# Gates scaled one stage ahead, and the merged product added in DRAM, in a retention and SSD hybrid block

## The chip, the cores and the metric

The kernel runs on one core of one Trainium2 chip. The metric is the device time of one execution in microseconds (us), as the median of several runs.

## The reference

One layer on x of 512 positions by 2048 channels, all in float32. A normalized x is projected to the inputs of two branches and to two gates. The retention branch gives y_r (2048 channels), the SSD branch y_s (4096 channels, normalized over its channels). What the change touches is the end:

```
y_s = rmsnorm(y_s * silu(z), ssd_norm_w)
p_r = y_r @ w_br_ret          # 2048 -> 2048
p_s = y_s @ w_br_ssd          # 4096 -> 2048
merged = sigmoid(gate_r) * p_r + sigmoid(gate_s) * p_s
x = x + merged @ w_out        # 2048 -> 2048
return rmsnorm(x, norm_f_w)
```

The kernel doesn't scale y_s by its norm's root before the product. Since the root R2 depends on the position alone, it multiplies the gate instead: sigmoid(gate_s) * R2 * p_s.

## The kernel before

Activations lie with channels on the 128 partitions and the 512 positions along the row. A float32 product is made of three fast ones: each operand is split into a high part (a cast to float32r) and a low part (the difference), for weights by `split` (L147: ScalarE writes whi, L148; VectorE writes wlo, L149), for activations by `first_half` and `second_half` (L169 and L179), which leave the operands a0 to a7 and b0 to b7.

A **unit** (`unit`, L258) makes 256 output channels from 2048 input channels: eight **slabs** of 256 input channels each. Weights come in pairs of slabs (wf, L235, SyncE's queue, three buffers). In most units a seven-product scheme (Strassen-like, `SEVEN`) is used, for which VectorE makes three differences per pair (L238, L240, L241); units 0 and 7 of the stages discussed here (`PLAIN2`) use the plain scheme. Each slab has 21 matmuls of 128 x 256 in a seven-product unit; the first five slabs run one after the other, the last three group by group (groups of 9, 6 and 6). Units alternate between the PSUM tiles pb and att. At a unit's end ScalarE and VectorE gather the products into o (L269 to L278).

The last four stages each have eight units (two output tiles, called rows, j = 2i and 2i + 1, to a unit):

- the retention product, whose rows are multiplied by the gate gr_d and stored to m_d (L714, L715);
- **half 1** of the SSD product (input channels 0 to 2047), whose rows are stored to ps_d (L726); ahead of it R2 is computed (L718, L719, and L310 to L314);
- **half 2** (channels 2048 to 4095), L728 to L742: for each row SyncE loads ps_d, gs_d (the sigmoid gate) and m_d into tiles f; GpSimd multiplies the gate by R2 (L737); VectorE adds the product to ps (L738), multiplies by the gate (L739) and adds m (L740); ScalarE's queue stores the result to mm_d (L742). The last two rows stay in SBUF;
- the output projection, whose operands are mm_d's rows (L743, loaded by L205), with L173 to L176 for the first halves and L182 to L187 for the second.

The tile f is shared by all loads of these stages and has four buffers; a load waits until the buffer's last user is done, and where that is a store, until it has landed. It stands meanwhile at the head of SyncE's queue:

```
def rtile(src, j, t=None):
    if t is None:
        t = bp.tile([P, T], F32, name="f", tag="f", bufs=4)
    SP.dma_start(out=t, in_=src[j * P:(j + 1) * P, :])
    return t
```

A scheduler in the framework sets the order of each engine's instructions when the program is built, from its own model of times and from priorities (weights go ahead). Each engine, and each queue of transfers, works in that order. The names stay, but the orders move wherever the code changes.

Of the kernel before, what the change touches and what calls it, by code (L numbers as in the profile page):

```python
# [8 lines left out]
F32 = mybir.dt.float32  # L9
# [3 lines left out]
ALU = mybir.AluOpType  # L13
# [3 lines left out]
P = 128  # L17
T = 512
TB = T // P
D = 2048  # L20
# [4 lines left out]
SW = 4096  # L25
# [75 lines left out]
NP = KD // 2  # L101
# [26 lines left out]
def hybrid_block(tc, A, out):  # L128
    nc = tc.nc
    PE, ACT, DVE, POOL, SP = nc.tensor, nc.scalar, nc.vector, nc.gpsimd, nc.sync  # L130
# [6 lines left out]
    op = ctx.enter_context(tc.tile_pool(name="op", bufs=2))  # L137
    dp = ctx.enter_context(tc.tile_pool(name="dp", bufs=1, space=DRAM))
# [5 lines left out]
    def att_tile():  # L144
        return att.tile([P, T], F32, name="att")
# [11 lines left out]
    def raw_tile(i):  # L157
        R[i] = hp.tile([P, 6, 256], F32, name=f"r{i}", tag=f"b{i}")
        return R[i][:, 0:4, :].rearrange("p (r h) t -> p r (h t)", r=2)
# [9 lines left out]
    def first_half(i, DVE=DVE, ACT=ACT):  # L169

        f, t = R[i], hp.tile([P, 8, 256], F32R, name=f"a{i}", tag=f"a{i}")
        X[i] = [t, None]
        DVE.tensor_tensor(f[:, 4, :], f[:, 0, :], f[:, 1, :], op=ALU.subtract)  # L173
        ACT.copy(t[:, 0:4, :], f[:, 1:5, :])
        yield
        DVE.tensor_tensor(t[:, 4:8, :], f[:, 1:5, :], t[:, 0:4, :].bitcast(F32), op=ALU.subtract)  # L176
        yield
# [12 lines left out]
    def second_halves(room):  # L190
        for i in range(NP):
            list(second_half(i, room[i % 2]))
# [4 lines left out]
    def rows(src, i):  # L197
        return src[i * 256:(i + 1) * 256, :].rearrange("(r p) t -> p r t", p=P)

    def load_operands(src, n=NP):  # L200


        for i in range(NP):
            if i < n:
                SP.dma_start(out=raw_tile(i), in_=rows(src, i))  # L205
            list(first_half(i))
# [90 lines left out]
    gs_d = dp.tile([D, T], F32, name="gs_d")  # L297
    ps_d = dp.tile([D, T], F32, name="ps_d")
    m_d = dp.tile([D, T], F32, name="m_d")
    mm_d = dp.tile([D, T], F32, name="mm_d")  # L300
    A_d = dp.tile([SH, T], F32, name="A_d")
    E_d = dp.tile([SH, T], F32, name="E_d")

# [3 lines left out]
    def inverse_root(dst, ps, y, z, n, DVE=DVE, ACT=ACT):  # L307


        ACT.activation(y, ps, AF.Abs_reciprocal_sqrt, scale=1.0 / n, bias=eps)  # L310
        DVE.tensor_scalar(z, ps, 1.0 / n, EPS, op0=ALU.mult, op1=ALU.add)
        DVE.tensor_tensor(dst, y, y, op=ALU.mult)
        DVE.scalar_tensor_tensor(dst, dst, -0.5, z, op0=ALU.mult, op1=ALU.mult)
        DVE.scalar_tensor_tensor(dst, dst, 1.5, y, op0=ALU.add, op1=ALU.mult)  # L314

    bg_ctx = ExitStack()
# [75 lines left out]
    ps = att_tile()  # L392
# [98 lines left out]
    with tc.tile_pool(name="ret", bufs=1) as rp:  # L491
# [3 lines left out]
        for h in range(NH):  # L495
# [45 lines left out]
            for sb in range(TB):  # L541
                n = T - sb * P
                ps = att_tile()
                for i in range(2):
                    PE.matmul(ps[:, :n], k[:, i, sb * P:(sb + 1) * P], q[:, i, sb * P:], start=(i == 0), stop=(i == 1))  # L545
                t = pts[:, (4 * sb - sb * (sb - 1) // 2) * P:][:, :n]
# [10 lines left out]
            for lb in range(TB):  # L557
                ps = att_tile()
# [22 lines left out]
    with tc.tile_pool(name="ssd", bufs=1) as sp:  # L581
# [23 lines left out]
        def gates(off, dst, i):  # L605
            w = w_in[:, off + i * 256:off + (i + 1) * 256]
            for e, x in enumerate(unit([w], plain=(2 * i + (off == GSO)) in PLAIN_M)):
                ACT.activation(x, x, AF.Sigmoid)
                ACT.dma_start(out=dst[(2 * i + e) * P:(2 * i + e + 1) * P, :], in_=x)

        todo = [(o, d, i) for i in range(NG) for o, d in ((GRO, gr_d), (GSO, gs_d))]
        for g in range(NG):
# [3 lines left out]
            ps = att_tile()  # L616
# [3 lines left out]
            ps = att_tile()  # L620
# [6 lines left out]
            for jj in range(2):  # L627
# [5 lines left out]
                for e in range(2):  # L633
                    j = j0 + e
# [7 lines left out]
                    ps = att_tile()  # L642
                    for c in range(TB):
# [6 lines left out]
                                       op=ALU.mult)  # L650
                    ps = att_tile()
# [5 lines left out]
                    for c in range(1, TB - 1):  # L657
                        for i in range(2):
# [8 lines left out]
                                 in_=A_d[hs, :].partition_broadcast(P))  # L667
# [27 lines left out]
                    gates(*todo.pop(0))  # L695
        gates(*todo.pop(0))
    sst_ctx.close()


    with tc.tile_pool(name="br", bufs=1) as bp:  # L700
        def rtile(src, j, t=None):
            if t is None:
                t = bp.tile([P, T], F32, name="f", tag="f", bufs=4)
            SP.dma_start(out=t, in_=src[j * P:(j + 1) * P, :])
            return t

        load_operands(yr_d)
        for i in range(NP):
            if i == 1:
                second_halves([bp.tile([P, 3, 256], F32, name="g", bufs=2) for n in range(2)])  # L710
            for e, x in enumerate(unit([w_r[:, i * 256:(i + 1) * 256]], i % 2, i in PLAIN2)):
                j = 2 * i + e
                t = rtile(gr_d, j)
                DVE.tensor_tensor(t, t, x, op=ALU.mult)  # L714
                ACT.dma_start(out=m_d[j * P:(j + 1) * P, :], in_=t)  # L715
        R2 = R1
        ps = att_tile()
        PE.matmul(ps, ones, R1, start=True, stop=True)  # L718
        inverse_root(R2, ps, *(bp.tile([P, T], F32, name="f", tag="f", bufs=4) for i in range(2)), SW)  # L719
        load_operands(ys_d[:D, :])  # L720
        for i in range(NP):
            if i == 1:
                second_halves([bp.tile([P, 3, 256], F32, name="g", bufs=2) for n in range(2)])
            for e, x in enumerate(unit([w_s[:D, i * 256:(i + 1) * 256]], i % 2, i in PLAIN2)):
                j = 2 * i + e
                ACT.dma_start(out=ps_d[j * P:(j + 1) * P, :], in_=x)  # L726
        load_operands(ys_d[D:, :])
        for i in range(NP):  # L728
            if i == 1:
                second_halves([bp.tile([P, 3, 256], F32, name="g", bufs=2) for n in range(2)])  # L730
            if i == NP - 1:
                last = raw_tile(i)
            for e, x in enumerate(unit([w_s[D:, i * 256:(i + 1) * 256]], i % 2, i in PLAIN2)):
                j = 2 * i + e
                p = rtile(ps_d, j, last[:, e, :] if i == NP - 1 else None)
                s, m = rtile(gs_d, j), rtile(m_d, j)
                POOL.tensor_tensor(s, s, R2, op=ALU.mult)  # L737
                DVE.tensor_tensor(p, p, x, op=ALU.add)  # L738
                DVE.tensor_tensor(p, p, s, op=ALU.mult)  # L739
                DVE.tensor_tensor(p, p, m, op=ALU.add)  # L740
                if i < NP - 1:
                    ACT.dma_start(out=mm_d[j * P:(j + 1) * P, :], in_=p)  # L742
        load_operands(mm_d, NP - 1)  # L743
    bg_ctx.close()


    with tc.tile_pool(name="fin", bufs=1) as fp:
# [4 lines left out]
        for i in range(NP - 1):  # L752
            if i == 1:
                second_halves([xo[n].rearrange("p r (h t) -> p (r h) t", h=2)[:, 0:3, :] for n in (5, 6)])
            t = xo[i]
            SP.dma_start(out=t, in_=rows(A["xT"], i))
            for e, x in enumerate(unit([w_o[:, i * 256:(i + 1) * 256]], i % 2, i in PLAIN2)):
                j = 2 * i + e
# [9 lines left out]
        t = xo[NP - 1]  # L768
        for e in range(2):
            j = KD - 1 - e  # L770
# [4 lines left out]
        ps = [att_tile()[:, :256] for h in halves]  # L775
# [78 lines left out]
```

## Time and profile before

| | |
|---|---|
| time, median of 3 runs | 2753.27 us (2751.96 to 2756.13) |
| the profiled execution's own time | 2755.9 us |
| its span | 2754.0 us |
| granted TensorE clock, mean | 0.993 |
| moved by DMA | 362.46 MB, 132 GB/s in the mean |

PE is TensorE's matmuls and PEld its weight loads, DVE is VectorE, ACT ScalarE, POOL GpSimd, SP SyncE; a q behind a name is that engine's queue, in which transfers are issued and waits are stood out. "x <- y" after a group names who ended most of its idle time. Rows of windows give a stretch, its length, then the busy time and count of each engine, the granted clock, the share of DMA and GB/s. Times in rows are us from the start of the span.

### The profile page before, as it was taken

The numbers are of one execution on the slowest core, as the hardware profiler recorded it, in microseconds if no ns is written. First come the engines' busy times: TensorE is split into PE (matmuls) and PEld (weight loads), VectorE is DVE, ScalarE is ACT, GpSimd is POOL, SyncE is SP. The second block draws the span as 40 slices with busy tenths as digits, with TensorE's granted clock in tenths as the row PEclk, the third lists the DMA queues.
The fourth block names the chain that finished last, engine by engine and source line by source line (L and its number), as shares of the span: only waits on it lengthen the run. The fifth ranks groups of instructions, "written<-read, shape, count | busy, mean of one in ns | idle before, by whom it ended". The sixth has DMA issues, their size and how long they took to land.

```text
span 2754.0 us, 51975 instructions
## 1 busy us (share of the span) xinstructions
PE 2691.5 (98%) x20448; PEld 2565.0 (93%) x20448; DVE 2368.3 (86%) x3799; ACT 1342.7 (49%) x1923; POOL 179.3 (7%) x130
## 2 busy tenths in 40 slices
PE   7999999999999999999999999999999999999998
PEld 4899999999999999999999999999999999898897
DVE  7998888888869898888989898898989897898997
ACT  4434333433345555565565555566564353433443
POOL 0000000000000000000000000000000000011221
PEclk9999999999999999999999999999999999999999
DMA  4223333333333444343444434343464644557534
GB/s 156 85 89 108 100 104 104 104 93 104 104 113 121 129 129 129 107 129 114 131 127 134 138 107 125 119 136 121 129 202 154 212 140 131 176 182 226 193 120 138
DMA packets 339766, 362.46 MB, mean 132 GB/s; under 512 B 25152, under 2 KB 297792, under 8 KB 339520
## 3 DMA queue, kind: packets, MB, share of 16 engines
q1 hardware_dynamic: 319136, 325.05, 38.2%
q10 hardware_dynamic: 20384, 34.09, 3.3%
q8 instruction: 160, 2.62, 0.4%
q14 instruction: 86, 0.70, 0.1%
HBM read 321.56 MB, written 37.49 MB: 130 GB/s over the span
## 4 chain that ended last, share of the span: by engine, by line
PE 78%; DVE 9%; DMA 6%; issue 3%; ACT 1%; SPq 1%; POOL 0%; DVEq 0%; ACTq 0%; POOLq 0%
PE pb L223 21%; PE pb L221 21%; PE pb L222 21%; DMA wf<-in_w_in_dram 3%; DVE wlo L149 3%; PE att L222 2%; PE att L223 2%; PE att L221 2%; PE att L545 1%; DVE wf L238 1%; PE att L560 1%; PE att L677 1%; DMA wf<-in_w_br_ssd_dram 1%; PE att L681 1%; PE pb L118 1%
## 5 line engine op out<-in xcount | busy, mean ns | idle before, releaser
L148 ACT CAST whi<-wf 128x896 fp32r<-128x896 f32 (+1 forms) x968 | 817.6, 884 | 908.2 <-PE pb L222 370.4
L149 DVE TENSOR_TENSOR wlo<-wf,whi 128x896 fp32r<-128x896 f32 (+1 forms) x968 | 988.3, 1033 | 57.2 <-ACT whi L148 35.6
L221 PE MATMUL pb<-a,whi 128*128 128x256 f32 (+1 forms) x3328 | 998.3, 303 | 7.7 <-DVE o L277 4.3
L223 PE MATMUL pb<-a,wlo 128*128 128x256 f32 (+1 forms) x3328 | 994.5, 301 | 7.2 <-DVE wlo L149 7.1
L222 PE MATMUL pb<-a,whi 128*128 128x256 f32 (+1 forms) x3328 | 996.8, 300 | 0.0
L221 PEld LDWEIGHTS pb<-a,whi 128*128 128x128 f32 x3328 | 636.0, 191 | 32.3 <-issue 7.4
L223 PEld LDWEIGHTS pb<-a,wlo 128*128 128x128 f32 x3328 | 635.2, 191 | 30.4 <-DVE wlo L149 8.9
L222 PEld LDWEIGHTS pb<-a,whi 128*128 128x128 f32 x3328 | 637.1, 191 | 20.3 <-issue 0.2
L221 PE MATMUL pb<-b,whi 128*128 128x256 f32 x2112 | 600.1, 284 | 0.0
L223 PE MATMUL pb<-b,wlo 128*128 128x256 f32 x2112 | 599.0, 284 | 0.0
L222 PE MATMUL pb<-b,whi 128*128 128x256 f32 x2112 | 598.1, 284 | 0.0
L238 DVE TENSOR_TENSOR wf<-wf 128x512 f32<-128x512 f32 x400 | 286.1, 715 | 173.9 <-DMA wf<-in_w_in_dram 133.0
L221 PEld LDWEIGHTS pb<-b,whi 128*128 128x128 f32 x2112 | 405.8, 192 | 0.1
L222 PEld LDWEIGHTS pb<-b,whi 128*128 128x128 f32 x2112 | 405.8, 192 | 0.0
L223 PEld LDWEIGHTS pb<-b,wlo 128*128 128x128 f32 x2112 | 405.5, 192 | 0.2
L241 DVE TENSOR_TENSOR wf<-wf 128x256 f32<-128x256 f32 x400 | 174.9, 437 | 3.2
L240 DVE TENSOR_TENSOR wf<-wf 128x256 f32<-128x256 f32 x400 | 174.3, 436 | 3.5
L223 PE MATMUL att<-a,wlo 128*128 128x256 f32 (+1 forms) x480 | 144.5, 306 | 5.1 <-DVE wlo L149 5.1
L221 PE MATMUL att<-a,whi 128*128 128x256 f32 (+1 forms) x480 | 145.2, 305 | 0.0
L222 PE MATMUL att<-a,whi 128*128 128x256 f32 (+1 forms) x480 | 145.2, 305 | 0.0
L223 PEld LDWEIGHTS att<-a,wlo 128*128 128x128 f32 x480 | 90.8, 192 | 10.3 <-DVE wlo L149 6.5
L221 PEld LDWEIGHTS att<-a,whi 128*128 128x128 f32 x480 | 92.0, 192 | 3.9
(217 smaller groups left out, 2731.5 us busy)
## 6 DMA issues: line engine op xcount, KB each, us to landing
wf<-in_w_in_dram SPq DMA_DIRECT2D x640, 256.0 KB, 3.1
wf<-in_w_br_ssd_dram SPq DMA_DIRECT2D x128, 256.0 KB, 3.3
wf<-in_w_out_dram SPq DMA_DIRECT2D x72, 256.0 KB, 3.1
wf<-in_w_in_dram SPq DMA_DIRECT2D x128, 128.0 KB, 2.6
L<-A_d SPq DMA_DIRECT2D x32, 512.0 KB, 3.7
wf<-in_w_br_ret_dram SPq DMA_DIRECT2D x64, 256.0 KB, 3.4
ys_d<-B ACTq DMA_DIRECT2D x32, 256.0 KB, 2.0
r<-ys_d SPq DMA_DIRECT2D x16, 512.0 KB, 6.6
```

Source lines behind the costliest of these rows:

```text
L118: ins = getattr(self.engine, name)(*args, **kw).ins
L148: ACT.copy(dst_hi, src)
L149: DVE.tensor_tensor(dst_lo, src, dst_hi.bitcast(F32), op=ALU.subtract)
L221: PE.matmul(o, wh, xh, start=b not in started, stop=False, skip_group_check=True)
L222: PE.matmul(o, wh, xl, start=False, stop=False, skip_group_check=True)
L223: PE.matmul(o, wl, xh, start=False, stop=(k == NP - 1), skip_group_check=True)
L238: DVE.tensor_tensor(f2[:, :, 4:6, :], f2[:, :, 1:3, :], f2[:, :, 0:1, :].to_broadcast([P, 2, 2, P]), op=ALU.subtract)
L240: DVE.tensor_tensor(f2[:, :, 0, :], f2[:, :, 2, :], f2[:, :, 4, :], op=ALU.add)
L241: DVE.tensor_tensor(f2[:, :, 6, :], f2[:, :, 3, :], f2[:, :, 0, :], op=ALU.subtract)
L545: PE.matmul(ps[:, :n], k[:, i, sb * P:(sb + 1) * P], q[:, i, sb * P:], start=(i == 0), stop=(i == 1))
L560: PE.matmul(ps[:, :DK], pt[sb][:, (lb - sb) * P:(lb - sb + 1) * P], v[:, sb, :], start=(sb == 0), stop=(sb == lb))
L677: PE.matmul(pi[i * 64:(i + 1) * 64, c * P:(c + 1) * P], xd[:, c, i, :], L[:, i, c, :], start=True, stop=True)
```

## The change

Four edits. The product gate * R2 moves from half 2 to half 1: there each row's gate is loaded, multiplied by GpSimd and stored back to gs_d through ScalarE's queue. In half 2 the rows 0 to 13 are no longer added to m by VectorE and stored to mm_d; GpSimd's queue writes them to m_d by a transfer that adds to what lies there. mm_d is gone, and the output projection reads m_d. Rows 14 and 15 load m and are added on VectorE as before. The tile f has six buffers in place of four, and the pool bg is closed ahead of these stages.

```
-    mm_d = dp.tile([D, T], F32, name="mm_d")
...
     sst_ctx.close()
+    bg_ctx.close()
...
-                t = bp.tile([P, T], F32, name="f", tag="f", bufs=4)
+                t = bp.tile([P, T], F32, name="f", tag="f", bufs=6)
...
                 ACT.dma_start(out=ps_d[j * P:(j + 1) * P, :], in_=x)
+
+                s = rtile(gs_d, j)
+                POOL.tensor_tensor(s, s, R2, op=ALU.mult)
+                ACT.dma_start(out=gs_d[j * P:(j + 1) * P, :], in_=s)
...
                 p = rtile(ps_d, j, last[:, e, :] if i == NP - 1 else None)
-                s, m = rtile(gs_d, j), rtile(m_d, j)
-                POOL.tensor_tensor(s, s, R2, op=ALU.mult)
+                s = rtile(gs_d, j)
                 DVE.tensor_tensor(p, p, x, op=ALU.add)
                 DVE.tensor_tensor(p, p, s, op=ALU.mult)
-                DVE.tensor_tensor(p, p, m, op=ALU.add)
                 if i < NP - 1:
-                    ACT.dma_start(out=mm_d[j * P:(j + 1) * P, :], in_=p)
-        load_operands(mm_d, NP - 1)
-    bg_ctx.close()
+                    POOL.dma_start(out=m_d[j * P:(j + 1) * P, :], in_=p, accum_op=ALU.add)
+                else:
+                    DVE.tensor_tensor(p, p, rtile(m_d, j), op=ALU.add)
+        load_operands(m_d, NP - 1)
```

Line numbers after the change differ by up to three. The scheduler's orders move at three places that matter.

ScalarE's queue at the start of half 1, where unit 0 is gathered (o<-pb) and the weights of unit 1 are cast. Before:

```order
L148 CAST whi<-wf 128x896 x2
L269 COPY o<-pb_25010 128x512
L185 CAST b_25202<-g 128x768
L148 CAST whi<-wf 128x896 x2
L269 COPY o<-pb_25012 128x512
L148 CAST whi<-wf 128x896 x2
L726 DMA ps_d<-o 128x512 x2
L148 CAST whi<-wf 128x896 x4
```

And now:

```order
L269 COPY o<-pb_25010 128x512
L185 CAST b_25210<-g 128x768
L148 CAST whi<-wf 128x896
L730 DMA gs_d<-f 128x512
L148 CAST whi<-wf 128x896
L730 DMA gs_d<-f 128x512
L269 COPY o<-pb_25012 128x512
L730 DMA gs_d<-f 128x512 x3
L148 CAST whi<-wf 128x896 x2
L730 DMA gs_d<-f 128x512 x2
L726 DMA ps_d<-o 128x512
L730 DMA gs_d<-f 128x512
```

Stores of the scaled gates now stand between the casts, and each waits for GpSimd's product.

SyncE's queue in half 2, from the loads of weights for units 0 to 2 on. Before:

```order
L235 DMA wf<-in_w_br_ssd_dram 128x2x256 x18
L704 DMA f<-gs_d 128x512
L704 DMA f<-m_d 128x512
L235 DMA wf<-in_w_br_ssd_dram 128x2x256
L704 DMA f<-ps_d 128x512
L235 DMA wf<-in_w_br_ssd_dram 128x2x256 x3
```

And now:

```order
L235 DMA wf<-in_w_br_ssd_dram 128x2x256 x18
L704 DMA f<-ps_d 128x512
L704 DMA f<-gs_d 128x512
L704 DMA f<-ps_d 128x512
L704 DMA f<-gs_d 128x512
L235 DMA wf<-in_w_br_ssd_dram 128x2x256 x8
```

Before, the loads between the weights are of the rows 1 and 2; now they are of the rows 3 and 4, since the rows 0 to 2 are loaded in half 1, and four pairs of weights follow on without a load between them.

GpSimd's queue at the end of the program. Before:

```order
L649 TENSOR_TENSOR xl<-xd,sst 128x384 x2
L691 TENSOR_TENSOR R_81<-R_81,B_8475 128x512 x2
L737 TENSOR_TENSOR f<-f,R_81 128x512 x16
L764 TENSOR_TENSOR R_81<-R_81,o 128x512 x13
L850 UNCONDITIONAL_BRANCH
```

And now:

```order
L648 TENSOR_TENSOR xl<-xd,sst 128x384 x2
L690 TENSOR_TENSOR R_81<-R_81,B_8474 128x512 x2
L729 TENSOR_TENSOR f<-f,R_81 128x512 x16
L744 DMA m_d<-f 128x512 x14
L767 TENSOR_TENSOR R_81<-R_81,o 128x512 x13
```

The sixteen products stand ahead of all fourteen adding transfers, in half 1 as the first excerpt shows.

More of the change, by code (lines that the diff above doesn't have):

```diff
@@ L718, in hybrid_block @@
         PE.matmul(ps, ones, R1, start=True, stop=True)
-        inverse_root(R2, ps, *(bp.tile([P, T], F32, name="f", tag="f", bufs=4) for i in range(2)), SW)
+        inverse_root(R2, ps, *(bp.tile([P, T], F32, name="f", tag="f", bufs=6) for i in range(2)), SW)
         load_operands(ys_d[:D, :])
```

## The prediction

> **What bounds the kernel now.** I read the page first, then the busy time of each engine in stretches cut by stage and by unit, then TensorE's waits, the chain of waits through the longest of them, and last VectorE's groups and SyncE's waits in the stage that the change edits.
>
> The page's first part says who is busy.
>
> ```profile
> PE 2691.5 (98%) x20448; PEld 2565.0 (93%) x20448; DVE 2368.3 (86%) x3799; ACT 1342.7 (49%) x1923; POOL 179.3 (7%) x130
> ```
>
> TensorE is the bound, so only its stalls can be won. Windows cut where the matmuls' tile changes between pb and att (units alternate) show them. The first two rows are the two halves of the SSD projection, which do the same matmuls; the third is the first three units of the output projection.
>
> ```profile
> 2217.41:2382.81 165.40, 165.40 (x1204) 157.37 (x1202) 134.67 (x208) 68.47 (x89) 2.05 (x1) 1.00 0.48 158
> 2382.81:2563.38 180.57, 169.66 (x1201) 159.70 (x1200) 161.86 (x245) 69.67 (x91) 23.04 (x14) 0.98 0.61 198
> 2563.38:2634.31 70.93, 66.46 (x434) 61.48 (x432) 68.00 (x108) 35.76 (x48) 25.02 (x4) 0.95 0.49 163
> ```
>
> The columns are length, then PE, PEld, DVE, ACT, POOL busy, clock, DMA share. Half 1 has no TensorE idle at all; half 2 takes 180.57 - 165.40 = 15.2 us longer. By units:
>
> ```profile
> 2217.41:2240.07 22.66, 22.66 (x100) 18.40 (x98) 22.66 (x39) 13.00 (x18) 0.00 (x0) 1.00 0.28 93
> 2240.07:2260.22 20.15, 20.15 (x169) 20.15 (x168) 17.95 (x27) 7.40 (x9) 2.05 (x1) 1.00 0.64 203
> 2260.22:2280.38 20.16, 20.16 (x170) 20.16 (x169) 16.65 (x26) 7.41 (x9) 0.00 (x0) 1.00 0.42 138
> 2405.53:2428.07 22.54, 20.92 (x170) 20.31 (x168) 22.13 (x33) 9.44 (x13) 1.31 (x1) 1.00 0.46 148
> 2513.64:2541.59 27.95, 22.91 (x170) 22.46 (x169) 22.20 (x36) 9.21 (x13) 2.59 (x2) 0.88 0.86 278
> ```
>
> An undisturbed unit of 168 matmuls takes 20.16 us (0.12 us each), a plain one 22.66. The unit from 2513.64 loses 7.8 us, and its clock of 0.88 says that part of that is matmuls at a lower clock after the stall. The output stage's first three units should take 22.66 + 2 x 20.16 = 62.98; they take 70.93, so 7.9 us are lost there. Winnable in all: 15.2 + 7.9 = 23.1 us.
>
> What TensorE waited for from 2382.8 to 2634, all four rows:
>
> ```profile
> PE pb L223 <- DVE wlo L149: 6.6, 4, 4.1
> PE att L223 <- DVE wlo L149: 5.1, 6, 1.9
> PE att L222 <- DVE b L187: 1.9, 1, 1.9
> PE att L221 <- ACT b L185: 1.7, 2, 1.1
> ```
>
> All of it is operands that VectorE (or ScalarE behind it) prepares. The chain through the 4.1 us wait:
>
> ```profile
> 2516.07 6.24 DMA mm_d<-f
> 2522.33 0.34 SPq L704
> 2522.76 4.01 DMA r<-mm_d
> ...
> 2529.10 1.09 DVE wlo L149
> 2530.24 0.80 PE pb L223 x2
> ```
>
> SyncE stood on the load of a tile f whose buffer was still being stored to mm_d (6.24 us); operands and weights queued behind it came late. So two causes share half 2's loss: a full VectorE, and the f buffers that hold up SyncE.
>
> **The change part by part.** VectorE's groups in half 2 (first six rows), and those rows of half 1 that are to be compared (last three):
>
> ```profile
> L149 DVE TENSOR_TENSOR wlo<-wf,whi 128x896 fp32r<-128x896 f32 x48 | 52.9, 1117 | 0.0
> L240 DVE TENSOR_TENSOR wf<-wf 128x256 f32<-128x256 f32 x24 | 11.7, 489 | 0.0
> L740 DVE TENSOR_TENSOR f<-f 128x512 f32<-128x512 f32 x14 | 11.1, 796 | 0.7 <-DMA f<-m_d 0.7
> L241 DVE TENSOR_TENSOR wf<-wf 128x256 f32<-128x256 f32 x24 | 10.7, 446 | 0.0
> L739 DVE TENSOR_TENSOR f<-f 128x512 f32<-128x512 f32 x14 | 9.6, 684 | 6.5 <-POOL f L737 6.5
> L738 DVE TENSOR_TENSOR f<-f,o 128x512 f32<-128x512 f32 x14 | 9.1, 681 | 0.3 <-DMA f<-ps_d 0.3
> ```
> ```profile
> L149 DVE TENSOR_TENSOR wlo<-wf,whi 128x896 fp32r<-128x896 f32 x48 | 51.4, 1084 | 0.7 <-ACT whi L148 0.6
> L240 DVE TENSOR_TENSOR wf<-wf 128x256 f32<-128x256 f32 x24 | 11.2, 465 | 0.3
> L241 DVE TENSOR_TENSOR wf<-wf 128x256 f32<-128x256 f32 x24 | 10.1, 419 | 0.3
> ```
>
> *Half 2, VectorE.* Removed: 14 adds of m (L740) at 0.68 us (L738's price) = 9.5 us; the waits for GpSimd's products, 6.5 us, and for m, 0.7. GpSimd's 14 products also lengthened VectorE's own instructions: L740 14 x (796 - 681), L149 48 x (1117 - 1084), L240 24 x 24, L241 24 x 27 ns = 1.6 + 1.6 + 0.6 + 0.6 = 4.4 us, or 0.31 us a product. Relief: 9.5 + 6.5 + 0.7 + 4.4 = 21 us. Busy time falls from 161.86 to 161.86 - 9.5 - 4.4 = 148, against 134.67 in half 1, which stalls nowhere.
>
> *Half 2, SyncE.*
>
> ```profile
> SPq L704 <- DMA mm_d<-f: 25.6, 10, 5.7
> ```
>
> Three tiles per row of output in four buffers become two in six, so a load now waits for the transfer of three tiles earlier. These 25.6 us shrink, but what they wait for changes: the buffer of p is free only when its adding transfer has landed, and no row shows one. Nearest are the plain transfers of the same 256 KB, m's load and mm_d's store (the first row, a weight load, is used below; the last column is us from issue to landing):
>
> ```profile
> wf<-in_w_br_ssd_dram SPq DMA_DIRECT2D x128, 256.0 KB, 3.3
> ```
> ```profile
> f<-m_d SPq DMA_DIRECT2D x16, 256.0 KB, 4.6
> ...
> mm_d<-f ACTq DMA_DIRECT2D x14, 256.0 KB, 4.4
> ```
>
> From below 4.4 us; from above, if reading the destination and writing it go one after the other, 4.4 + 4.6 = 9.0. I take 7, between them, as it does the work of both in one transfer. Below 4.4 is excluded, since it moves no less than the store. The Trainium skill, DMA: Bandwidth & Descriptors, section on the anatomy of a GpSimd-path DMA, gives 2.0 us + bytes/436e3, an estimate of 2.6 us for 256 KB; by it SyncE would be free 4 us sooner and the sum about 1 us lower, 2740. The plain stores here take 4.4, more than that fit, so the trace decides.
>
> What is behind such a load is weights. SyncE comes to the first p loads of half 2 when the eight weight loads of this row are issued, at 2415.7:
>
> ```profile
> 2399.06 16.61 SPq L235 DMA_DIRECT2D wf<-in_w_br_ssd_dram  x8
> ```
>
> In the change the p loads of rows 3 and 4 stand there, waiting for the adding transfers of rows 0 and 1 (a row is one j, a tile of 128 channels). Before, the first p * s was written here:
>
> ```profile
> L739 DVE TENSOR_TENSOR f<-f x14: 676/681/693, 2417.5 to 2558.1; 128x512 f32<-128x512 f32 x14
> ```
>
> Row 0 is done at 2418.2, row 1 some 1.5 us later; with 7 us to land, SyncE is free at about 2427. The next weight pair is the third of unit 2, used at 2405.53 + 20.16 + 4 x 2.52 = 2435.8; its load takes 3.3 us, and differences, cast and subtraction (L240, L241, L149 above, the cast further down) some 4, so it must be issued by 2428.5. It just fits at 7 us; at 9 about 1 us is lost every second unit.
>
> On GpSimd's queue only further adding transfers stand behind one that waits for its p. The last of them (rows 12 and 13) is waited for by the load of the seventh operand, which the output stage needs five slabs into its first unit, a whole plain unit (22.66 us) after the rows are done, so at 7 us it is hidden.
>
> Half 2 then keeps about 4 of its 15.2 us (VectorE still at 148 of 167, SyncE just in time): a gain of 11, bounds 6 and 15.2.
>
> *Output stage.* The same queues carry over: rows 12 and 13 lose their m adds, rows 14 and 15 keep the old path (the m load stays, the product is ready). VectorE enters with 2 x 0.68 us less and no wait for the last products (L737 to 2566.0). The b operands that TensorE waits for come from a VectorE that is full there (68.00 of 70.93), so a part stays: I take half, 4 of 7.9; bounds 0 and 7.9.
>
> *Half 1, the price.* Sixteen loads, products and stores of the gates move here, all beside its first three units by the order of the queues. The products can start when the norm's root is done:
>
> ```profile
> 2234.59 0.68 DVE L314 SCALAR_TENSOR_TENSOR R<-R,f 128x512 f32<-128x512 f32 x1
> ```
> ```profile
> L737 POOL TENSOR_TENSOR f<-f,R x16: 1287/1505/2142, 2254.5 to 2564.7; 128x512 f32<-128x512 f32 x16
> ```
>
> Sixteen products at 1.5 to 2.1 us run from 2235.3 to 2259 or 2269, in units where VectorE is full or nearly so (22.66 of 22.66, then 17.95 of 20.15). ScalarE's queue holds the stores between weight casts: the stores of rows 2 to 4 stand ahead of the casts that start at 2242.36 below. Row 4's product ends about 2235.3 + 5 x 1.7 = 2243.8, so these casts come 1.5 us late; the next four stand behind the stores of rows 5 to 8, whose last product ends at 2250.6.
>
> ```profile
> 2242.36 1.78 ACT L148 CAST whi<-wf 128x896 fp32r<-128x896 f32 x2 [2.38 <-issue]
> ```
> ```profile
> 2253.30 2.09 DVE L149 TENSOR_TENSOR wlo<-wf,whi 128x896 fp32r<-128x896 f32 x2
> 2255.30 1.52 DVE L240 TENSOR_TENSOR wf<-wf 128x256 f32<-128x256 f32 x1
> ```
>
> The first of that wlo pair is the last slab of the unit from 2240.07: ready about 2254.4, used after five slabs of 21 matmuls and two groups of 9, at 2240.07 + 123 x 0.12 = 2254.8. The margin is 0.4 us, so a lateness there comes out nearly whole. Nine products by then cost VectorE 9 x 0.31 = 2.8 us, or, if each blocks like the one in the L240 row (1.52 against 0.42), 9 x 1.10 = 9.9; 1.8 us of idle ahead of the pair absorbs some. I take 3 us, nearer the low end, since fourteen products in an equally full half 2 averaged 0.31; bounds 0 and 10.
>
> *Sum, on the profiled execution:* its 2755.9 us (span 2754.0 and 1.9 around it) is 2.6 above the median of 2753.27, so I carry the difference over: -11 - 4 + 3 = -12, that is 2743.9 there and 2741.3 beside the median, rounded 2741. Closing the pool bg earlier costs nothing: it can make the first tiles of br wait for the last head's store, beside a unit of the retention product whose operands are loaded; without that cover it is one store's landing, under 4.4 us. About 0.2%, 5.5 us, is what a measurement of this kernel tells from no change.
>
> **The rivals.**
>
> *Products stop VectorE in half 1.* For it: the 1.10 us above, and the margin of 0.4 us. All sixteen at that price are 17.6 us; VectorE's idle in the units from 2240.07 and 2260.22 is 2.2 + 3.5 = 5.7. Half 1 would lose up to 12, say 10: net -11 - 4 + 10 = -5, 2748. Against: the average of 0.31. The Trainium skill, SBUF — State Buffer, section "Who interferes with whom", speaks against the change here: a VectorE instruction with two SBUF inputs and a GpSimd one that reads SBUF exclude each other for a whole instruction. The 1.10 us of lengthening agrees with it; the average says that it strikes only sometimes.
>
> *Adding transfers land slowly: the change is slower.* From the sum above, weights are late once an adding transfer takes over 8 us, and each us beyond is paid every second unit, three times in six units. At 14 us: 3 x 6 = 18 on top of -12, net +6, 2759; the sign turns at 12 us. For it: nothing in the trace does such a transfer, and DMA is 0.61 busy in half 2. Against: 12 us is more than m's load and mm_d's store in turn, 9.0.
>
> *Half 2 stays tied to weight loads.* VectorE gets its 21 us but waits for weights that SyncE loads when wlo frees them; then only the chains through mm_d go, about the 7.8 us of one unit, and half 1 costs its 3: net -5, 2748. For it: SyncE's queue is in order either way. Against: half 1 has the same coupling and no stall.
>
> **How the numbers follow.** Forecast 0.57; products stopping VectorE 0.17; slow adding transfers 0.14; tied to weights 0.12. The forecast's own bounds are -15.2 - 7.9 + 0 = -23 and -6 - 0 + 3 = -3; I cut the best case to -22, 2731. Above, the range takes in the two cases at 2748 and part of the slow-transfer case, to 2757; what is left out is about 2 in 10. Faster by over 0.2% (under 2747.8): nearly all of the forecast (0.53), half of each case at 2748 (0.08 + 0.05): 0.66 less 0.01 for caution. Slower by over 0.2%: most of the slow transfers, 0.11, and 0.01. Same: the rest, 0.23.
>
> **What would show it.** Right: units of half 2 near 20.2 us, clock 1.00 in all, L739 without a wait for POOL; the adding transfers landing in about 7 us; the unit of half 1 that ends at 2260 some 3 us longer. Wrong: half 2 above 175 us; half 1 above 172 us with wlo or whi waits; SyncE's f loads waiting over 8 us for m_d.

## The result and the profile after

The change makes the kernel slower: 2758.36 us, median of 22 runs (2752.58 to 2763.19), against 2752.88 of 22 runs of before (2745.54 to 2757.35) beside them; ratio 1.0023, interval 1.0017 to 1.0029. The forecast was 2741, range 2731 to 2757.

The profiled execution, with 2752.6 us, is the fastest of the 22. So this profile alone cannot show where the lost 6 us are; against before's profiled execution (2755.9) it is even 3 us shorter. Its windows, cut as before's (columns as there: length, PE, PEld, DVE, ACT, POOL busy, clock, DMA share, GB/s): half 1, half 2, the output stage's first three units, and the second unit of half 1.

```profile
2215.97:2390.19 174.22, 168.07 (x1203) 159.03 (x1202) 153.35 (x218) 72.23 (x93) 30.73 (x16) 0.99 0.61 203
2390.19:2559.56 169.37, 166.25 (x1201) 157.34 (x1200) 138.72 (x217) 65.79 (x87) 12.31 (x14) 1.00 0.66 184
2559.56:2631.62 72.06, 65.31 (x433) 59.63 (x432) 69.77 (x111) 33.36 (x45) 21.42 (x2) 0.98 0.47 161
2238.63:2267.60 28.97, 22.82 (x169) 21.80 (x168) 27.89 (x24) 7.24 (x9) 24.36 (x14) 0.94 0.84 287
```

Half 1 has lost 8.8 us (165.40 before), all of it in its second unit (20.15 before). Half 2 has won 11.2, the output stage lost 1.1.

**Half 1.** GpSimd's products in the after profile, and VectorE's groups in that unit:

```profile
L729 POOL TENSOR_TENSOR f<-f,R x16: 1276/1738/5338, 2235.3 to 2270.9; 128x512 f32<-128x512 f32 x16
```
```profile
L149 DVE TENSOR_TENSOR wlo<-wf,whi 128x896 fp32r<-128x896 f32 x9 | 14.6, 1632 | 1.0 <-ACT whi L148 0.9
L240 DVE TENSOR_TENSOR wf<-wf 128x256 f32<-128x256 f32 x3 | 4.3, 1431 | 0.1
```

The products start from 2235.3 to 2270.9, and the first takes 5.3 us beside a full VectorE. VectorE's wlo takes 1632 ns in place of 1084, its difference of L240 1431 in place of 465. Over half 1, each instruction that overlaps a product compared with the median of its shape, the lengthening is 12.7 us for 16 products, 0.79 each. The Trainium skill, SBUF — State Buffer, section "Who interferes with whom", says that VectorE with two SBUF inputs and GpSimd's reads lock each other out for whole instructions; the 5.3 us and the 1431 ns agree with it. ScalarE's queue in that unit:

```profile
2241.07 0.94 ACT L148 CAST whi<-wf 128x896 fp32r<-128x896 f32 x1 [2.64 <-POOL f L729]
...
2248.75 1.78 ACT L148 CAST whi<-wf 128x896 fp32r<-128x896 f32 x2 [5.09 <-POOL f L729]
...
2256.25 1.78 ACT L148 CAST whi<-wf 128x896 fp32r<-128x896 f32 x2 [5.72 <-DMA gs_d<-f]
```

The casts of weights stand behind stores of products that aren't there yet. TensorE's waits in half 1, where before has none:

```profile
PE att L223 <- DVE wlo L149: 3.5, 3, 2.1
PE att L221 <- ACT whi L148: 2.7, 1, 2.7
```

So of the 8.8 us TensorE stands 3.5 for VectorE's wlo and 2.7 for a cast of ScalarE; the rest is matmuls at a lower clock (22.82 us busy in place of 20.15, granted clock 0.94). VectorE itself is busy 27.89 of the 28.97 us.

**Half 2.** The adding transfers' landing, their queue's share of the 16 DMA engines, and what SyncE and VectorE waited for there:

```profile
q0 software_dynamic: 2016, 3.67, 14.7%
...
m_d<-f POOLq DMA_DIRECT2D x14, 256.0 KB, 6.1
```
```profile
SPq L704 <- DMA m_d<-f: 23.7, 11, 4.2
```
```profile
DVE wf L238 <- DMA wf<-in_w_br_ssd_dram: 18.4, 11, 4.0
```

VectorE is busy 138.72 us in place of 161.86, but it now waits 18.4 us for weights, where before it waited 8.0:

```profile
DVE wf L238 <- DMA wf<-in_w_br_ssd_dram: 8.0, 8, 1.9
```

Not all of that is the adding transfers' doing: e2 below, which has none, waits 13.0 us there.

**Output stage.** TensorE's waits from 2390.2 to 2631.6, the first three of six rows, and the chain into the output stage's first unit:

```profile
PE att L223 <- DVE wlo L149: 4.4, 4, 2.1
PE pb L221 <- ACT a L174: 3.3, 1, 3.3
PE pb L221 <- ACT whi L148: 0.7, 1, 0.7
```

```profile
2550.34 7.45 DMA m_d<-f
2557.84 3.76 DMA r<-m_d
2561.97 0.68 DVE wlo L149
2562.65 1.14 DVE a L176
2564.23 0.70 DVE o L271
2564.95 0.70 DVE r L741
```

The last adding transfer isn't hidden: the seventh operand's load starts when it has landed, 2557.84, and VectorE stands 5.4 us on it in order. The 3.3 us that TensorE waits for an operand's cast (a, L174) are the end of that chain.

### The profile page after: what moved, and what is told of

Its sections match the earlier page's. It is cut to its first block, busy times and chain, and to the rows that moved or that the text cites. A ratio compares the mean times of both kernels' runs of the same rounds, so it can differ in the third digit from the quotient of the medians.

```text
span 2750.8 us, 51997 instructions
## 1 busy us (share of the span) xinstructions
PE 2689.5 (98%) x20448; PEld 2563.2 (93%) x20448; DVE 2364.4 (86%) x3785; ACT 1342.1 (49%) x1923; POOL 200.4 (7%) x144
## 3 DMA queue, kind: packets, MB, share of 16 engines
q0 software_dynamic: 2016, 3.67, 0.9%
## 4 chain that ended last, share of the span: by engine, by line
PE 77%; DVE 10%; DMA 6%; issue 4%; ACT 2%; POOL 1%; SPq 0%; DVEq 0%; ACTq 0%; POOLq 0%
PE pb L221 21%; PE pb L223 21%; PE pb L222 20%; DMA wf<-in_w_in_dram 3%; DVE wlo L149 3%; PE att L223 3%; PE att L221 2%; PE att L222 2%; DVE wf L238 1%; PE att L676 1%; PE att L559 1%; PE att L544 1%; DMA wf<-in_w_br_ssd_dram 1%; DMA m_d<-f 1%; PE pb L118 1%
## 5 line engine op out<-in xcount | busy, mean ns | idle before, releaser
L221 PE MATMUL pb<-a,whi 128*128 128x256 f32 (+1 forms) x3328 | 999.1, 303 | 12.9 <-DVE o L277 4.4
L223 PEld LDWEIGHTS pb<-a,wlo 128*128 128x128 f32 x3328 | 635.0, 191 | 23.7 <-DVE wlo L149 2.0
L240 DVE TENSOR_TENSOR wf<-wf 128x256 f32<-128x256 f32 x400 | 174.3, 436 | 3.3
```

Source lines behind the costliest of these rows:

```text
L221: PE.matmul(o, wh, xh, start=b not in started, stop=False, skip_group_check=True)
L223: PE.matmul(o, wl, xh, start=False, stop=(k == NP - 1), skip_group_check=True)
L240: DVE.tensor_tensor(f2[:, :, 0, :], f2[:, :, 2, :], f2[:, :, 4, :], op=ALU.add)
```

## The experiments

Each, e1 to e18, was timed in five rounds beside before. Stage lengths (us) are of one profile each, cut where the matmuls' tile changes.

| kernel | ratio to before | interval | half 1 | half 2 | output, 3 units |
|---|---|---|---|---|---|
| before, first profile | | | 165.4 | 180.6 | 70.9 |
| before again (e5) | 1.0005 | 0.9995 to 1.0014 | 165.4 | 172.6 | 68.9 |
| after, first profile | 1.0023 | 1.0017 to 1.0029 | 174.2 | 169.4 | 72.1 |
| after again (e4) | 1.0031 | 1.0019 to 1.0043 | 176.1 | 175.0 | 71.1 |
| e1 adding only | 1.0043 | 1.0027 to 1.0058 | 165.6 | 181.6 | 71.2 |
| e2 gates only | 1.0009 | 0.9998 to 1.0020 | 174.3 | 171.2 | 68.4 |
| e3 rows 12, 13 by hand | 1.0036 | 1.0023 to 1.0049 | 175.1 | 177.1 | 69.5 |
| e6 gates as a chain | 1.0007 | 0.9998 to 1.0016 | 168.2 | 176.7 | 68.3 |
| e7 eight buffers | 1.0031 | 1.0022 to 1.0040 | 179.9 | 173.8 | 70.0 |
| e8 no product | 1.0017 | 1.0008 to 1.0026 | 168.1 | 172.0 | 71.5 |
| e9 loads off SyncE | 1.0024 | 1.0014 to 1.0034 | 175.4 | 171.7 | 74.2 |
| e10 gates only, loads off | 1.0006 | 0.9996 to 1.0017 | 174.4 | 170.1 | 66.5 |
| e11 chain, loads off | 0.9999 | 0.9991 to 1.0008 | 167.1 | 169.6 | 72.4 |
| e12 the same, adding | 1.0028 | 1.0019 to 1.0038 | 165.5 | 176.3 | 73.5 |
| e13 plain stores | 1.0001 | 0.9992 to 1.0011 | 176.0 | 164.7 | 70.9 |
| e14 adding twice | 1.0075 | 1.0058 to 1.0092 | 174.0 | 178.7 | 72.8 |
| e15 chain, six buffers | 1.0007 | 0.9997 to 1.0016 | 171.2 | 172.5 | 66.7 |
| e16 before, loads off | 0.9987 | 0.9978 to 0.9996 | 165.4 | 170.5 | 72.2 |
| e17 the same again | 0.9990 | 0.9979 to 1.0001 | 165.4 | 168.7 | 72.6 |
| e18 chain, two buffers | 1.0027 | 1.0016 to 1.0037 | 176.1 | 173.4 | 71.1 |

**Which half of the change costs?** The first theory (A) was the products in half 1, its rival (B) the adding transfers. Adding only (e1) has the product back in half 2:

```
-                s = rtile(gs_d, j)
-                POOL.tensor_tensor(s, s, R2, op=ALU.mult)
-                ACT.dma_start(out=gs_d[j * P:(j + 1) * P, :], in_=s)
...
                 s = rtile(gs_d, j)
+                POOL.tensor_tensor(s, s, R2, op=ALU.mult)
```

> Half of the change: the adding transfers and six f buffers, with the products g_s*R2 left where they were, on GpSimd in half 2. Theory A (the products beside a full VectorE are what costs): half 1 is back at 165 us (after: 174.2), half 2 keeps the part of its gain that comes from the m adds and the mm_d chain and comes to about 175 (before 180.6, after 169.4), the output stage's first three units stay at 72; the whole about 2748, 5 below before. Theory B (the adding transfers are what costs, the products are harmless in the median): half 2 and the output stage come out longer than before, and the whole at 2757 or more.

Gates only (e2) has m, mm_d and ScalarE's store as before:

```
-                s = rtile(gs_d, j)
+                s, m = rtile(gs_d, j), rtile(m_d, j)
...
+                DVE.tensor_tensor(p, p, m, op=ALU.add)
...
-                    POOL.dma_start(out=m_d[j * P:(j + 1) * P, :], in_=p, accum_op=ALU.add)
+                    ACT.dma_start(out=mm_d[j * P:(j + 1) * P, :], in_=p)
```

> The other half of the change: the products g_s*R2 a stage ahead with their stores into gs_d, while m is added on VectorE and the sum stored plainly into mm_d by ScalarE, as before; six f buffers. Theory A: half 1 174 us, half 2 about 175 as the products are gone from it but the m adds stay, output stage 71 or less; the whole 2755 to 2758, 3 to 5 above before. Theory B: half 1 no more than 170 in a profile, half 2 170, output stage 69; the whole below 2750.

A's half 1 is right (165.6 without the products, 174.3 with them), but as the cause of the slower median A falls: e1, with no product in half 1, is the slower of the two. Most of the products' 9 us come back in half 2 and the output stage; the adding transfers bring nothing back: e1's half 2 takes 181.6, though VectorE is 10 to 13 us less busy there than in before's two profiles. B has e1 right and e2's half 2 and output stage nearly so (171.2, 68.4), but not e2's half 1. The two prices, 1.0009 and 1.0043, don't add up to the change's 1.0023 to 1.0031.

**How far one profile goes.** after and before were profiled once more.

> The changed kernel once more, for a second profile: the first profiled execution (2752.6) was the fastest of 22 with a median of 2758.4, so the 6 us that separate the medians cannot be seen in it. Theory A: an execution nearer the median has its extra time in half 1 (177 to 180 us in place of 174.2) as the products meet VectorE there. Theory C: it has it at the start of the output stage (75 or more in place of 72.1). If neither stage is longer and the time is spread over the whole program, the difference is one between executions, of before too, and only medians count.

> The kernel before against itself, for a second profile of it and to see what the comparison makes of no change: ratio 1.000 within 0.0015. Before's first profile (2755.9) was above most of its runs, so if medians are to be explained by stages, one that lies nearer its median must show half 1, half 2 and the first three units of the output stage together below the first profile's 416.9 us: 408 to 414. Half 1 has no tight place and stays 165.4; the difference lies in half 2 (180.6) or the output stage (70.9). If it lies ahead of half 1 instead, the stages around the change are read with an error of that size.

The same windows (half 1, half 2, output) of after again and of before again:

```profile
2213.16:2389.24 176.08, 168.93 (x1203) 158.96 (x1202) 155.72 (x218) 74.44 (x96) 30.54 (x16) 0.99 0.60 201
2389.24:2564.20 174.96, 167.95 (x1201) 158.89 (x1200) 139.77 (x219) 65.72 (x87) 12.34 (x14) 0.99 0.64 182
2564.20:2635.28 71.08, 65.55 (x433) 60.10 (x432) 69.33 (x110) 32.09 (x43) 17.60 (x1) 0.98 0.46 154
```
```profile
2215.21:2380.61 165.40, 165.40 (x1203) 157.37 (x1202) 138.99 (x215) 70.82 (x93) 2.09 (x1) 1.00 0.49 160
2380.61:2553.25 172.64, 167.14 (x1201) 158.57 (x1200) 158.84 (x239) 67.02 (x87) 23.16 (x14) 0.99 0.65 206
2553.25:2622.18 68.93, 65.43 (x434) 61.03 (x433) 66.30 (x106) 34.48 (x46) 23.62 (x3) 0.95 0.51 166
```

Half 1 hardly varies; half 2 varies by 6 to 8 us in both kernels. Before's two profiles differ by 12.2 us in span, and 9.9 of them lie in the two stages that the change was to mend. The means of two profiles, after less before: half 1 175.2 - 165.4 = +9.8, half 2 172.2 - 176.6 = -4.4, output 71.6 - 69.9 = +1.7: +7.1, near the medians' +5.5 and more (1.0023 and 1.0031).

**Half 1: lock or queues?** e8 drops the line `POOL.tensor_tensor(s, s, R2, op=ALU.mult)`.

> The changed kernel with the sixteen products on GpSimd left out: the gates are loaded and stored back unscaled in half 1, so the output misses the norm's scale; loads, stores, buffers and adding transfers are all as in after. Theory A, by the products themselves: half 1 165.4 to 167 us (after's two profiles 174.2, 176.1), half 2 and the output stage as in after; the whole 8 to 10 below after. Rival, by the queues: ScalarE's and SyncE's stores and loads of the gates among weight casts and weight loads keep costing, half 1 170 or more.

168.1 us, between the two: 2.7 of the cost are the stores and loads among the weights' casts and loads, the other 6 to 8 the products. Whether these cost by lengthening VectorE's instructions or by the casts that wait for them in ScalarE's queue, e8 can't tell, since it takes away both. The whole gains only 2 to 4 us on after, not 8 to 10. e6 (on e2) strings each gate's steps on GpSimd's queue:

```
-                s = rtile(gs_d, j)
+                s = bp.tile([P, T], F32, name="s", bufs=1)
+                POOL.dma_start(out=s, in_=gs_d[j * P:(j + 1) * P, :])
                 POOL.tensor_tensor(s, s, R2, op=ALU.mult)
-                ACT.dma_start(out=gs_d[j * P:(j + 1) * P, :], in_=s)
+                POOL.dma_start(out=gs_d[j * P:(j + 1) * P, :], in_=s)
```

> The gates-only kernel (m added on VectorE, mm_d as before), with each gate's load, product and store in half 1 all on GpSimd's queue with one buffer of their own, so that they follow one another about 10 us a row over the whole of half 1 and neither SyncE nor ScalarE has any part in them. Theory A, now for half 1 alone (16 products crowded into three units cost it 9 us, by VectorE's lengthening and by ScalarE and SyncE standing on them): half 1 165 to 167 us, half 2 171, output stage 68; the whole 8 below the gates-only kernel and 5 below before. Rival: a product costs TensorE about 0.55 us wherever it stands, half 1 stays at 173 or more and the whole within 2 of the gates-only kernel. A second rival: the chain is too slow, the last rows' gates come late, and half 2 loses what half 1 gains.

Half 1 comes to 168.2, just above the 165 to 167 expected, and to 167.1, 165.5, 171.2 and 176.1 in its descendants e11, e12, e15 and e18. In e11 VectorE is lengthened by 10.8 us (worked out as above), nearly the 12.7 of after, yet half 1 loses 1.7 us in place of 8.8. So the lengthening cost little where it was spread over eight units with idle time in each. That crowding alone makes the difference is not shown, since a chain also takes the stores out of ScalarE's queue and the loads out of SyncE's. And the second rival holds too: half 2's first unit takes some 26 us with a chain (e6, e11, e12, e18) in place of after's 21.8, and the whole stays at before's time, where 5 below was expected. e15 and e18 ask why.

> The kernel with the gates as a chain on GpSimd, no adding transfers and half 2's loads on GpSimd (it was at before's time, ratio 0.9999), with six f buffers beside the chain's own in place of five, which makes the scheduler order VectorE and ScalarE anew around half 2's first unit (25.6 us there, against 21.7 in the kernels without a chain). If the long first unit is a matter of that order: half 2 165 to 167 (169.4), the whole 2742 to 2744 beside before at 2747, faster. If it comes from the chain's last row (its transfers run until 2386): first unit again 25 or more and the whole at before's time within 2.

> Gates as a chain on GpSimd with two buffers of its own (loads overlap stores, some 6 us a row in place of 9.5, so that it ends near 2330 and not at 2386), half 2's loads on GpSimd, no adding transfers. If the long first unit of half 2 (25.6 us) came from the chain's last rows: 21.7 there, half 2 166, the whole 2741 to 2744 beside before at 2747. If it comes from the order in which VectorE and ScalarE stand there: 24 to 26 again and the whole at before's time within 2.

The first unit takes 22.1 us in e15 and 26.2 in e18, whose last product starts at 2318: it goes by the order, not by the chain's last rows. That unit in e11 and, without a chain, in e13:

```profile
2378.38:2404.09 25.71, 22.64 (x98) 17.86 (x96) 25.66 (x40) 14.21 (x20) 2.44 (x3) 1.00 0.39 123
2389.40:2411.16 21.76, 21.76 (x97) 18.02 (x96) 21.53 (x35) 12.51 (x18) 0.00 (x0) 1.00 0.35 114
```

VectorE is full in both, but with a chain it has 40 instructions to do there and not 35. Neither run is faster for it (1.0007, 1.0027). e15 loses 5 us in half 1's seventh unit, behind a weight load of 4.2 us; e18 loses 5 in the second, behind one of 6.4 us, and 4 in the fifth. VectorE is lengthened by 11.2 us in e18, as much as in e11, and half 1 loses 10.7, so the lengthening alone doesn't fix the cost. What made these loads late is open.

**Output stage: the last adding transfers.** e3 adds with `if i < NP - 2` and stores rows 12 and 13 plainly after VectorE's add.

> The changed kernel, but rows 12 and 13 get m on VectorE and a plain store, as rows 14 and 15 and all rows of before did; rows 0 to 11 keep the adding transfers. Theory C (the output stage waits for the last adding transfer, through the load of the seventh operand, which VectorE stands on in order): the seventh operand's load ends some 4 us earlier, the hole of 3.7 us on TensorE and the half clock behind it (3.4 us at half speed, 1.7 us) go: first three units of the output stage about 67 (after: 72.1), the whole about 2754, 4 to 5 below after. Rival: the m load and the store take as long as the adding transfer did, and VectorE's two adds come back; output stage 71 to 72 and the whole within 2 of after.

The hole on TensorE shrinks from 3.7 us (1.8 in after's second profile) to 1.1 and the stage by some 2, as theory C has it in kind, but not in size, and the whole shows nothing of it. The rival's part is right there.

**Half 2: SyncE, or the DMA engines?** e7 has `bufs=8`; e9 gives rtile a queue, `q.dma_start`, and passes POOL for half 2's loads; e10 does the same on e2.

> The changed kernel with eight f buffers in place of six, so that in half 2 the p load of a row takes the buffer of the row four before it (two units) in place of three. Theory D (what the adding transfers cost in half 2 goes through SyncE: 23.7 to 26.4 us of its time stand on f loads whose buffer an adding transfer still reads, and the weight loads behind come late): those waits go below 8 us, VectorE's waits for weights (18.4 to 21.5 us at its L238) fall to before's 8, half 2 comes to 166 to 170 (after's two profiles: 169.4, 175.0), and the whole to 4 to 8 below after. Rival: the buffers only move the wait, to L742 or to other loads, and the whole stays within 2 of after.

> The changed kernel, but half 2's loads of p and s (and m for rows 14 and 15) are issued by GpSimd, whose queue holds only the adding transfers there; SyncE keeps the weights and the operands. Eight buffers did not test theory D, because the scheduler sets f loads a row earlier as soon as there is a buffer, so that SyncE stands on the transfer just issued all the same (24.7 us in 12 waits). Theory D, tested by the queue: SyncE's waits for adding transfers go, VectorE's waits for weights at L238 fall from 17.7 to 21.5 us to below 8, half 2 comes to 164 to 168 (five profiles with adding transfers and no products there: 169.4 to 177.1, mean 173.4); the whole 5 to 8 below after. Rival: the adding transfers cost by moving 7.3 MB through the DMA engines in GpSimd's own queue, weights stay late, half 2 stays at 170 to 175.

> The gates-only kernel (no adding transfers; m added on VectorE) with half 2's loads of p, s and m issued by GpSimd. Theory D: the waits of SyncE for mm_d stores (17.3 us) go here as well, half 2 167 or less (171.2), output stage 68; the whole 3 to 5 below the gates-only kernel, that is at before's time or 2 below, and 5 or so below the changed kernel with the same edit, since the output stage keeps 68 against 71. Rival: without adding transfers SyncE was not late, and the edit changes nothing (within 2 of gates-only).

D falls as the whole cause. With eight buffers SyncE still stands 24.7 us on adding transfers, and half 2 (173.8) and the whole stay at after's, as the rival had it. e10 changes nothing either: 1.0006 beside e2's 1.0009, half 2 170.1 beside 171.2. In e9 SyncE's loads of p and s are gone from its queue and with them its waits for adding transfers in half 2, the ratio is still 1.0024, and VectorE still waits 20.9 us for weights. The chain of waits in e9 shows on what:

```profile
2512.87 0.34 DVE wf L241
2513.32 10.17 DMA wf<-in_w_br_ssd_dram
2523.55 0.57 issue
```

The weight load was issued at once and took 10.17 us; GpSimd had issued two adding transfers and two loads from 2511.08 to 2512.88. Taking issue and landing of all 64 weight loads of half 2 in the after profile, the 18 in flight beside an adding transfer take 6.4 us in the mean, the other 46 3.4; in before all 64 take 4.0, and the 32 beside one of mm_d's plain stores 4.6. So theory E: the adding itself holds the DMA engines. e13 drops only `accum_op=ALU.add`, and every engine's instructions stay in the same order.

> The changed kernel with plain stores in place of the adding transfers, from the same GpSimd queue, to the same rows of m_d, with every instruction on every engine in the same order: only the adding is left out, so rows 0 to 13 of the sum lack m. Theory E (the adding itself holds the DMA engines: 178 ns per 2 KB packet against 84, and weight loads in flight beside it land 3 us later): the stores land in 4 to 5 us (6.1), the weight loads beside them in about 4 (6.3), half 2 comes to 165 to 168 (169.4, 174.7), the output stage to 68 to 70 (72.2, 71.2), the whole 4 to 8 below after. Rival (it is the burst at a row's end, or the scheduled order, whatever the transfer does): weight loads beside the stores still take 5.5 or more, half 2 and the whole within 2 of after.

E's half 2 and whole come out (the whole 6 to 8 us below after). Its window, and the rows that answer to after's:

```profile
2389.40:2554.10 164.70, 164.70 (x1202) 157.05 (x1201) 140.71 (x221) 65.75 (x87) 7.76 (x14) 1.00 0.60 195
```
```profile
q0 software_dynamic: 1120, 3.67, 5.5%
...
m_d<-f POOLq DMA_DIRECT2D x14, 256.0 KB, 4.2
```
```profile
SPq L704 <- DMA m_d<-f: 14.4, 10, 2.8
```
```profile
DVE wf L238 <- DMA wf<-in_w_br_ssd_dram: 12.9, 11, 2.2
```

Half 2 has no TensorE idle left: 164.70 in place of 169.4 and 175.0. The same 3.67 MB take 5.5% of the engines' time in place of 14.7%. They also go in 1120 packets in place of 2016, so the run doesn't part the addition from the smaller packets that come with it. The weight loads beside the stores still take 5.4 us, where E expected 4: part of the delay is any burst at a row's end, as the rival had it. The output stage, 70.9, hardly gained, though TensorE no longer waits for a (L174) there. e14 adds every p a second time, `out=gr_d[j * P:(j + 1) * P, :], in_=p, accum_op=ALU.add`, into rows that nobody reads.

> The changed kernel with a second adding transfer of each p, into rows of gr_d that nobody reads any more: twice the adding traffic, the sum in m_d unchanged. Theory E: more weight loads meet one (18 of 64 in after), each lands some 3 us late or more, VectorE's waits for weights at L238 rise from 18 to 21 us to 30 or more, half 2 comes to 180 or more, the whole 6 to 12 above after. Rival (one transfer's cost is its own landing, which is waited for at the end of the stage and nowhere else): the second one, which nobody waits for, changes half 2 by less than 3.

```profile
q0 software_dynamic: 3886, 7.08, 25.9%
```
```profile
DVE wf L238 <- DMA wf<-in_w_br_ssd_dram: 28.4, 8, 6.9
```

Weight loads beside them take 7.0 us, half 2 comes to 178.7, just under the 180 expected, and the whole to 1.0075, 12 to 14 us above after. None, one, two: 12.9, 18.4 (21.5 in after's second profile) and 28.4 us of VectorE's waits. (The second transfer also holds p's buffer longer; SyncE stands 40.3 us on it.) The Trainium skill, DMA: Bandwidth & Descriptors, section "Issuing engines are not separate DMA queues", says that transfers of all queues run on the same 16 DMA engines; e9's 10.17 us, of a load on SyncE's queue beside adding ones on GpSimd's, agrees.

**A version that beats both?** e11 joins the chain and e10's loads; e12 is the same with adding transfers.

> The gates in half 1 as a chain on GpSimd (one buffer, a row each 8 to 10 us), no adding transfers, and half 2's loads on GpSimd as well. Half 1 168 as in the chain kernel (2.8 over before in place of 8.9), half 2 167 to 171, output stage 68: 404 to 407 for the three against 407 to 417 of before's two profiles; the whole 2742 to 2745 beside before at 2747, faster than both kernels. Rival: half 2's first units stay long (25.8 and 21.1 us in the chain kernel), because the order of ScalarE and VectorE there has changed and not because of SyncE; then the whole is 2748 or more.

> The whole change with both cures: gates in half 1 as a chain on GpSimd, adding transfers kept, half 2's loads on GpSimd. Theory (A for half 1, D for half 2, C for the output stage): half 1 168, half 2 164 to 168, output stage 71; 403 to 407 for the three, the whole 2741 to 2745 beside before at 2747, and within 2 of the chain kernel without adding transfers: what they take off VectorE in half 2 they give back in the output stage. If it is below that kernel by 3 or more, adding transfers pay once SyncE is out of their way; if above by 3 or more, they never pay here.

With adding 1.0028, without 0.9999: neither beats before. e11 has half 1 as expected, but half 2's first unit stays long, as the rival had it, and the output stage takes 72.4, not 68. Adding costs 8 us on top of e11, so it doesn't pay here even with SyncE out of its way. e16 is before with half 2's loads on GpSimd, nothing else; e17 repeats it.

> The kernel before with half 2's loads of p, s and m issued by GpSimd, between the products that GpSimd does there anyway; nothing else changed. If SyncE's standing on buffers (25.6 us behind mm_d stores, in 10 waits) made weights late in before: half 2 168 to 172 (180.4 and 172.4 in two profiles), the whole 3 to 6 below before. If VectorE's fill (162 of 180 busy) and its waits for the products are what bounds half 2: no change within 2; and slower by 3 or more if the loads, in order behind products, come late.

> Before with half 2's loads of p, s and m on GpSimd's queue, once more. If the gain of 0.13% is real: ratio again 0.997 to 0.9995, half 2 170 or less again (170.2), where before's two profiles have 180.4 and 172.4. If it was one lucky comparison among sixteen: ratio 0.9995 to 1.001 and half 2 somewhere in 170 to 180.

```profile
2381.51:2550.20 168.69, 165.75 (x1201) 157.26 (x1200) 154.83 (x236) 65.14 (x86) 48.95 (x53) 1.00 0.64 205
```

Half 2 of 170.5 and 168.7, against 180.6 and 172.6, is what was expected if SyncE was late in before too. That is argued, not shown: VectorE's work moved as well (236 instructions in half 2, in place of 245 and 239). 0.9987 and 0.9990, the second interval just reaching 1: some 3 us below before, 9 to 12 below the change.

## Why the prediction was wrong

The sum was -11 - 4 + 3. By the means of two profiles it came to -4.4 + 1.7 + 9.8, so that each of its three terms missed by 6 to 7 us.

- *Half 1, the price, +3.* The step that failed first, by size: +8.8 and +10.7. "I take 3 us, nearer the low end" used 0.31 us of lengthening a product, from the means of half 2, where products are two to a unit. Counted as for after, instruction by instruction, the same half 2 gives 0.43 (0.51 in before's second profile); crowded it was 0.79, against the upper 1.10. The place (the unit that ends at 2260, the casts behind the stores) was right, the lateness of the casts not: 2.6 to 5.7 us, not 1.5. The lower clock behind the stalls, 2.7 us, was not in the price.
- *Half 2, a gain of 11.* It met its own profile to 0.2 us, by luck: it was reckoned from a before of 180.57 whose second profile has 172.64, and after's second has 174.96. The mean gain is 4. The adding transfer was priced by when it lands (7; 6.1 measured) and by SyncE's standing on it. What it does to the weight loads beside it was not in the sum, and is what cost: without the addition e13 takes 164.7 in place of 172. VectorE's relief was real and not what ended last. Its busy time fell by 23 us (161.86 to 138.72) where 13.9 were reckoned, but of the 28 instructions fewer only 14 are adds of m, and half 1 has ten more (operand work such as L187's, nine in place of six).
- *Output stage, -4.* Failed: +1 to +2. "Hidden behind a plain unit" was wrong, since VectorE reaches the seventh operand in its order long before TensorE does, and stands 5.4 us. That is not the whole of it: e13, where TensorE's wait for that chain is gone, still takes 70.9. What else holds the stage is open.
- *What could be won.* The 23.1 us were taken from one profile. By before's second, 13.2 were there: 7.2 in half 2 and 6.0 in the output stage. In the same way the 2.6 us by which the profiled execution lay above the median were kept as a constant; 9.9 of the 12.2 us between the two profiles lie in the stages to be mended, so this was most likely part of the gain counted.
- *Rivals.* The products stopping VectorE had place and price (10) right, but kept the other two gains. Slow adding transfers had the sign, by another way: none took 12 us (7.9 at most in after's two profiles), the weights beside them were late all the same. Half 2 tied to weight loads had the wait right (VectorE stood 18.4 and 21.5 us on weights), but not its source: e13 keeps SyncE's order, waits 12.9 us, and TensorE has no idle.

## What to carry to other kernels

Price a transfer by the DMA engine time that it takes from the transfers beside it, not only by when it lands: an addition moved from VectorE into the transfers relieves an engine and loads a resource that the weights need. Work on GpSimd that lengthened VectorE by 11 to 13 us cost 1.7 us spread thinly with free queues (e11) and 8.8 crowded among stores and casts (after); price it by where it stands, not by an average. And take a stage's loss from two profiles before counting it as winnable.

## What the hardware showed beyond that

- An adding transfer takes 14.7 / 5.5 = 2.7 times the DMA engine time of the plain store of the same bytes (in 2016 packets against 1120 for the fourteen), lands in 6.1 us against 4.2, and holds GpSimd 0.86 us to issue against 0.54.
- One product on GpSimd beside a full VectorE took 5.3 us, the shortest 1.28.
- More buffers didn't lessen SyncE's waits (24.7 us with eight, 23.7 and 26.4 with six): the scheduler sets the loads one row earlier, and they wait for the transfer just issued.
